# Strassen's weight sums in an FFN: from GpSimd to accumulating transfers and VectorE

## The chip, the cores and the metric

The kernel runs on one core of a Trainium2 chip. The metric is the device time of one execution in microseconds. A core has five engines that concern us here: TensorE (PE, and PEld for its weight loads), VectorE (DVE), ScalarE (ACT), GpSimd (POOL) and SyncE (SP), which issues most transfers between DRAM and on-chip memory. They run side by side and wait for each other through semaphores; each runs its own instructions in order.

## The reference

One layer of a decoder, in float32, for a prompt of 512 tokens and for 8 sequences of one new token each, 520 tokens with shared weights, `D_MODEL` = 2048:

```python
h = modulate(rmsnorm(x, g_norm_mix), sh1, sc1)
x = x + gt1 * (concat([attention(h @ w_in), rwkv7(h @ w_in)]) @ w_out)
h2 = modulate(rmsnorm(x, g_norm_ffn), sh2, sc2)
gate, up = split(h2 @ w_ffn_in, 2)
x = x + gt2 * ((silu(gate) * up) @ w_ffn_out)
y = rmsnorm(x, g_norm_final)
```

The new keys, values and states are returned as well. The change lies in `h2 @ w_ffn_in`, with 2 x 5632 columns in `w_ffn_in`.

## The kernel before

Products are taken in three matmuls: weights and activations are each cut into a high half in TensorE's short float32 format (`wh`, a cast on ScalarE, line 1243) and the rest (`wl`, a subtraction on VectorE, line 1244), and wh·bH, wh·bL and wl·bH are summed in PSUM (`product`, lines 1395 to 1401). The 520 tokens are two halves of `HB` = 260 columns. Activations lie transposed: 128 rows of the model dimension on the partitions, tokens along the free axis.

The FFN's first projection (`ffn_in`) is one level of Strassen's scheme in Winograd's form. The weights of one hidden tile `ht` (128 gate columns and 128 up columns) are four blocks: A11 and A12 (gate, first and second half of the model dimension), A21 and A22 (up). The tokens are four blocks too: B11, B21 (first token half, upper and lower half of the model dimension), B12, B22 (second token half). Instead of eight products of blocks there are seven, over sums:

- sums of weights: S1 = A21 + A22, S2 = S1 - A11, S3 = A11 - A21, S4 = A12 - S2
- differences of tokens: T1 = B12 - B11, T2 = B22 - T1, T3 = B22 - B12, T4 = T2 - B21
- products: A11·B11, A12·B21, S1·T1, S2·T2, S3·T3, A22·T4, S4·B22

The loop runs over 44 hidden tiles and, in each, over two halves `g` of the inner dimension (4 blocks of 128 rows each). Per half SP loads the four blocks of 128x512 weights (256 KB each, `load`: tiles `sr` for A11, A21, A12 with six buffers, `raw` for A22 with three), GpSimd forms the four sums in place (lines 1430, 1431 and 1435, 1436, or 1441, 1442 where the first two products were taken early), and TensorE runs seven products of 12 matmuls, 84 matmuls a half and 168 a tile. The tile names in the program are a11, a21 (first A21, then S1), s3 (with the name tag `ar`), a11 again for S2 and a12 again for S4. At the end of a tile the sums of products (lines 1455 to 1463) are formed on VectorE from PSUM, ScalarE takes the silu (1464), VectorE multiplies (1465), and GpSimd's queue stores the tile of 128x520 in DRAM (`gd`, 1467).

The token differences are formed while the stage starts (`norm_second`): eight pairs of blocks are normalized (VectorE, line 1234; ScalarE, 1238; a small copy on GpSimd, 1236), three of four differences per pair of pairs run on GpSimd (1273, 1278, 1282), one on VectorE (1280), and each result is cut into its two halves. Meanwhile TensorE takes the first two products of hidden tiles 0 to 2, which need only B11 and B21 ("early", 144 matmuls); hidden tiles 0 to 2 then have five products a half.

The order of the instructions on each engine is not the program's order: a scheduler in the tile framework sets it when the kernel is built, from its own prices and from when buffers come free. So an edit in one line can move others. After the stage comes the output projection (`ffn_out`).

Of the kernel before, what the change touches and what calls it, by code (L numbers as in the profile page):

```python
# [10 lines left out]
ALU = mybir.AluOpType  # L11
# [7 lines left out]
HB = 260  # L19
# [44 lines left out]
class Kern:  # L64
# [1197 lines left out]
    def norm_second(self, psum):  # L1262

        nc = self.nc
        r = self.norm(1, psum("ssq2"), nc)
        us = self.norm_start(nc, 1, r)
        yield
        sub = ALU.subtract
        put = lambda f, kp, src: self.cut(nc, f[kp][:, 0], f[kp][:, 1], src)
        for kp in range(4):  # L1270
            b11, b21 = self.hb0[kp], self.hb0[kp + 4]
            b12 = self.norm_pair(nc, 1, kp, r, us)
            nc.gpsimd.tensor_tensor(b11, b12, b11, sub)
            yield
            b22 = self.norm_pair(nc, 1, kp + 4, r, us)
            put(self.T1, kp, b11)
            yield
            nc.gpsimd.tensor_tensor(b12, b22, b12, sub)
            put(self.B22, kp, b22)
            nc.vector.tensor_tensor(b22, b22, b11, sub)  # L1280
            yield
            nc.gpsimd.tensor_tensor(b21, b22, b21, sub)
            put(self.T2, kp, b22)
            yield
            for f, src in ((self.T3, b12), (self.T4, b21)):
                f.append(self.xp.tile([P, 2, 2, HB], F32R, tag="x", bufs=8, name=self.nm("xT")))
                put(f, kp, src)
            yield
# [76 lines left out]
    def ffn_in(self, st):  # L1365

        tc, nc, I = self.tc, self.nc, self.I
        mt = lambda nm: self.ps_m.tile([P, 2, 512], F32, tag="m", name=self.nm(nm))  # L1370
        fb = self.fpb.enter_context(tc.tile_pool(name="fpb", bufs=1, side="right"))
        quads = lambda n: [fb.tile([P, 2, 2, HB], F32R, name=f"{n}_{i}") for i in range(4)]
        self.B22, self.T1, self.T2 = quads("B22"), quads("T1"), quads("T2")
        self.T3, self.T4 = [], []
        plain = lambda k0: lambda k: [a[:, k0 + k] for a in self.B0]
        quad = lambda f: lambda k: [f[k // 2][:, i, k % 2] for i in range(2)]
        B11, B21 = plain(0), plain(8)
        B22, T1, T2, T3, T4 = map(quad, (self.B22, self.T1, self.T2, self.T3, self.T4))
        sp = self.fpb.enter_context(tc.tile_pool(name="strw", bufs=1))
        ct = lambda tag, n: sp.tile([P, 2, HB], F32, tag=tag, bufs=n, name=self.nm(tag))  # L1380
        src = lambda ht, row, col, g: I["w_fi"][2 * ht + row][:, 1024 * col + 512 * g:1024 * col + 512 * g + 512]

        def load(ht, row, col, g, tag="sr"):
            pool, n = (self.w, 3) if tag == "raw" else (sp, 6)
            t = pool.tile([P, 512], F32, tag=tag, bufs=n, name=self.nm(tag))
            nc.sync.dma_start(t, src(ht, row, col, g))
            return t

        def weights(t):
            wh, wl = (self.w.tile([P, 512], F32R, tag=n, bufs=3, name=self.nm(n)) for n in ("wh", "wl"))  # L1390
            self.cut(nc, wh, wl, t)
            return wh, wl

        def product(ps, w, b, g):
            wh, wl = w
            for k in range(4):
                s = slice(k * 128, k * 128 + 128)
                bH, bL = b(4 * g + k)
                for i, (x, y) in enumerate(((wh, bH), (wh, bL), (wl, bH))):
                    nc.tensor.matmul(ps[:, :HB], x[:, s], y, start=g == k == i == 0,  # L1400
                                     stop=g == 1 and k == 3 and i == 2, skip_group_check=True)

        def first_sums(pc, ps):
            nc.scalar.copy(pc[:, 1], ps[:, 0, :HB])
            nc.vector.tensor_tensor(pc[:, 0], ps[:, 1, :HB], pc[:, 1], ALU.add)

        norm = self.norm_second(lambda nm: mt(nm)[:, 0])
        early = []
        for ht in range(3):
            ps = mt("pm")  # L1410
            for g in range(2):
                for col, b in enumerate((B11, B21)):
                    product(ps[:, col], weights(load(ht, 0, col, g, "raw")), b, g)
                    next(norm, None)
            pc = ct("pc", 3)
            first_sums(pc, ps)
            early.append(pc)
        self.kept = []
        for ht in range(FT):
            pc = early.pop(0) if early else None  # L1420
            old = pc is not None
            if not old:
                pc, p12 = ct("pc", 3), mt("pm")
            p45, p67, p3 = mt("pm"), mt("pm"), mt("pm")
            for g in range(2):
                a11, a21 = load(ht, 0, 0, g), load(ht, 1, 0, g)
                a22 = load(ht, 1, 1, g, "raw")
                a12 = load(ht, 0, 1, g)
                s3 = self.w.tile([P, 512], F32, tag="ar", bufs=3, name=self.nm("s3"))
                nc.gpsimd.tensor_tensor(s3, a11, a21, ALU.subtract)  # L1430
                nc.gpsimd.tensor_tensor(a21, a21, a22, ALU.add)  # L1431
                if not old:
                    product(p12[:, 0], weights(a11), B11, g)
                    w2 = weights(a12)
                    nc.gpsimd.tensor_tensor(a11, a21, a11, ALU.subtract)  # L1435
                    nc.gpsimd.tensor_tensor(a12, a12, a11, ALU.subtract)
                    product(p12[:, 1], w2, B21, g)
                    if g == 1:
                        first_sums(pc, p12)
                else:  # L1440
                    nc.gpsimd.tensor_tensor(a11, a21, a11, ALU.subtract)
                    nc.gpsimd.tensor_tensor(a12, a12, a11, ALU.subtract)
                if ht == 0 and g == 0:
                    for _ in range(12):
                        next(norm, None)
                for ps, a, b in ((p45[:, 1], a21, T1), (p67[:, 0], a11, T2), (p67[:, 1], s3, T3),
                                 (p45[:, 0], a22, T4), (p3[:, 0], a12, B22)):
                    product(ps, weights(a), b, g)
                    if ht == 0 and g == 0:
                        next(norm, None)  # L1450
                        next(norm, None)
                    if g == 0:
                        continue
                    if b is T2:
                        nc.vector.tensor_tensor(pc[:, 1], p67[:, 0, :HB], pc[:, 1], ALU.add)
                    elif b is T3:
                        cu = ct("cu", 2)
                        nc.vector.tensor_tensor(cu[:, 1], p67[:, 1, :HB], pc[:, 1], ALU.add)
                    elif b is T4:
                        nc.vector.tensor_tensor(cu[:, 0], cu[:, 1], p45[:, 0, :HB], ALU.subtract)  # L1460
                        nc.vector.tensor_tensor(pc[:, 1], p45[:, 1, :HB], pc[:, 1], ALU.add)  # L1461
                        nc.vector.tensor_tensor(cu[:, 1], p45[:, 1, :HB], cu[:, 1], ALU.add)  # L1462
            nc.vector.tensor_tensor(pc[:, 1], p3[:, 0, :HB], pc[:, 1], ALU.add)  # L1463
            nc.scalar.activation(pc, pc, AF.Silu)
            nc.vector.tensor_tensor(cu, pc, cu, ALU.mult)
            if ht < FT - 4:
                nc.gpsimd.dma_start(self.gd[ht], cu)
            else:
                gs = [self.fp.tile([P, 2, HB], F32R, tag="n", bufs=self.nb, name=self.nm("g" + c)) for c in "HL"]
                self.cut(nc, gs[0], gs[1], cu)  # L1470
                self.kept.append([a.unsqueeze(1) for a in gs])
        self.fpb.close()
# [212 lines left out]
```

## Time and profile before

| | |
|---|---|
| runs of the kernel before | 2715.43, 2715.49, 2721.11 us; median 2715.49 |
| the profiled execution | 2716.84 us |
| its span in the profile | 2714.9 us |
| TensorE busy | 2586.2 us (95%) |
| VectorE busy | 1824.8 us (67%) |
| ScalarE busy | 1109.9 us (41%) |
| GpSimd busy | 808.4 us (30%) |

The profile shows one execution. The time beyond the span, 1.9 us, lies before the first and after the last instruction that it records. Shares of busy time are means over the whole span; matmuls are pipelined, so that their durations of some 280 ns overlap, and how fast TensorE goes is read from how many start in a stretch of time. A wait is put down to the event that came last.

### The profile page before, as it was taken

The numbers are of one execution on the slowest core, as the hardware profiler recorded it, in microseconds if no ns is written. First come the engines' busy times: TensorE is split into PE (matmuls) and PEld (weight loads), VectorE is DVE, ScalarE is ACT, GpSimd is POOL, SyncE is SP. The second block draws the span as 40 slices with busy tenths as digits, with TensorE's granted clock in tenths as the row PEclk, the third lists the DMA queues.
The fourth block names the chain that finished last, engine by engine and source line by source line (L and its number), as shares of the span: only waits on it lengthen the run. The fifth ranks groups of instructions, "written<-read, shape, count | busy, mean of one in ns | idle before, by whom it ended". The sixth has DMA issues, their size and how long they took to land.

```text
span 2714.9 us, 59056 instructions
## 1 busy us (share of the span) xinstructions
PE 2586.2 (95%) x23405; PEld 2369.0 (87%) x23405; DVE 1824.8 (67%) x3637; ACT 1109.9 (41%) x2142; POOL 808.4 (30%) x755
## 2 busy tenths in 40 slices
PE   6899999999999999985999999999999999999997
PEld 4577778788787898885999999999999999999997
DVE  2466677767756364688888888888888863444457
ACT  3133455544423344464444444444444432222225
POOL 0012121211212000066655556555655510000004
PEclk9899999999989998997999999999999999999999
DMA  7965454555556752252333333333333262432433
GB/s 270 326 197 172 139 155 140 154 160 158 158 175 202 235 171 88 96 169 94 132 113 115 109 121 108 116 110 114 117 110 117 98 200 91 125 124 91 125 102 110
DMA packets 203381, 387.24 MB, mean 143 GB/s; under 512 B 29616, under 2 KB 40800, under 8 KB 203072
## 3 DMA queue, kind: packets, MB, share of 16 engines
q1 hardware_dynamic: 193392, 353.10, 40.0%
q0 software_dynamic: 9072, 29.32, 3.5%
q8 instruction: 183, 3.00, 0.4%
q10 hardware_dynamic: 640, 1.05, 0.2%
q14 instruction: 94, 0.77, 0.1%
HBM read 350.92 MB, written 33.46 MB: 142 GB/s over the span
## 4 chain that ended last, share of the span: by engine, by line
PE 45%; DVE 4%; issue 2%; ACT 1%; POOL 1%; DMA 0%; DVEq 0%; SPq 0%; POOLq 0%; ACTq 0%
PE pm L1400 27%; PE pf L98 18%; DVE wl L1244 2%; ACT wh L1243 1%; DVE pc L1463 1%; DVE cu L1460 1%; DVE pc L1461 0%; POOL sr L1435 0%; DMA gr<-gd 0%; POOL sr L1431 0%; DVE x L1546 0%; PE ssq L1214 0%; DVE cu L1462 0%; DVE rstdh L1217 0%; DVEq L1681 0%
## 5 line engine op out<-in xcount | busy, mean ns | idle before, releaser
L1244 DVE TENSOR_TENSOR wl<-sr,wh 128x512 fp32r<-128x512 f32 x428 | 471.1, 1115 | 99.9 <-ACT wh L1243 83.1
L88 ACT CAST wh<-raw 128x512 fp32r<-128x512 f32 (+2 forms) x411 | 250.0, 611 | 496.7 <-PE pf L98 281.0
L1243 ACT CAST wh<-sr 128x512 fp32r<-128x512 f32 x428 | 265.2, 620 | 365.8 <-PE pm L1400 272.1
L98 PE MATMUL pf<-go,wh 128*128 128x260 f32 x2560 | 414.2, 282 | 0.0
L91 DVE TENSOR_TENSOR wl<-raw,wh 128x512 fp32r<-128x512 f32 (+2 forms) x411 | 287.6, 702 | 177.6 <-ACT wh L88 170.9
L98 PEld LDWEIGHTS pf<-go,wh 128*128 128x128 f32 x2560 | 353.9, 188 | 0.1
L98 PE MATMUL pm<-hH,wh 128*128 128x260 f32 (+1 forms) x1248 | 296.7, 317 | 2.0 <-ACT hH L143 1.6
L1400 PE MATMUL pm<-T,wh 128*128 128x260 f32 x1408 | 263.3, 285 | 8.0 <-ACT wh L1243 8.0
L98 PE MATMUL pf<-go,wl 128*128 128x260 f32 x1280 | 267.9, 282 | 0.0
L98 PE MATMUL pm<-hL,wh 128*128 128x260 f32 (+1 forms) x1248 | 264.3, 291 | 0.2 <-DVE hL L144 0.2
L98 PE MATMUL pm<-hH,wl 128*128 128x260 f32 (+1 forms) x1248 | 261.8, 290 | 0.0
L1400 PE MATMUL pm<-xT,wh 128*128 128x260 f32 x1408 | 261.7, 286 | 0.0
L98 PEld LDWEIGHTS pm<-hH,wh 128*128 128x128 f32 (+1 forms) x1248 | 195.1, 191 | 50.6 <-issue 32.0
L1400 PEld LDWEIGHTS pm<-T,wh 128*128 128x128 f32 x1408 | 219.9, 191 | 8.4 <-ACT wh L1243 8.4
L1400 PEld LDWEIGHTS pm<-xT,wh 128*128 128x128 f32 x1408 | 217.1, 189 | 3.9
L1400 PE MATMUL pm<-B0H,wl 128*128 128x260 f32 x704 | 205.7, 292 | 14.3 <-DVE wl L1244 14.3
L1400 PE MATMUL pm<-T,wl 128*128 128x260 f32 x704 | 203.5, 289 | 12.6 <-DVE wl L1244 12.6
L1400 PE MATMUL pm<-B0H,wh 128*128 128x260 f32 x704 | 200.8, 285 | 7.6 <-ACT wh L1243 6.5
L98 PEld LDWEIGHTS pm<-hL,wh 128*128 128x128 f32 (+1 forms) x1248 | 197.1, 191 | 5.6 <-issue 2.3
L98 PEld LDWEIGHTS pm<-hH,wl 128*128 128x128 f32 (+1 forms) x1248 | 197.0, 191 | 5.7 <-issue 1.8
L98 PEld LDWEIGHTS pf<-go,wl 128*128 128x128 f32 x1280 | 201.0, 188 | 0.0
L1400 PE MATMUL pm<-B0L,wh 128*128 128x260 f32 x704 | 199.6, 284 | 0.0
(420 smaller groups left out, 5484.1 us busy)
## 6 DMA issues: line engine op xcount, KB each, us to landing
sr<-in_w_fi SPq DMA_DIRECT2D x264, 256.0 KB, 2.7
ar<-in_w_ada SPq DMA_DIRECT2D x256, 256.0 KB, 3.1
raw<-in_w_fo SPq DMA_DIRECT2D x176, 256.0 KB, 2.6
raw<-in_w_in SPq DMA_DIRECT2D x148, 256.0 KB, 3.6
araw<-in_w_ada SPq DMA_DIRECT2D x64, 512.0 KB, 6.6
raw<-in_w_fi SPq DMA_DIRECT2D x100, 256.0 KB, 3.1
raw<-in_w_out SPq DMA_DIRECT2D x74, 256.0 KB, 3.1
gd<-cu POOLq DMA_DIRECT2D x40, 260.0 KB, 2.7
```

The source lines that it names most:

```text
L88: nc.scalar.copy(wh[:, :n], raw[:, :n])
L91: nc.vector.tensor_tensor(wl[:, :n], raw[:, :n], wh[:, :n].bitcast(F32), ALU.subtract)
L98: nc.tensor.matmul(ps[:m, bank, :HB], w, a[:, k, h, :], start=first and i == 0, stop=last and i == 2, skip_group_check=True,)
L1243: nc.scalar.copy(H, src)
L1244: nc.vector.tensor_tensor(L, src, H.bitcast(F32), ALU.subtract)
L1400: nc.tensor.matmul(ps[:, :HB], x[:, s], y, start=g == k == i == 0, stop=g == 1 and k == 3 and i == 2, skip_group_check=True)
L1460: nc.vector.tensor_tensor(cu[:, 0], cu[:, 1], p45[:, 0, :HB], ALU.subtract)
L1463: nc.vector.tensor_tensor(pc[:, 1], p3[:, 0, :HB], pc[:, 1], ALU.add)
```

## The change

The sums of weights leave GpSimd. S3 is loaded as A11 by SP (new line 1430) and A21 is added to it by a transfer from DRAM that accumulates into on-chip memory (1432); S1 is A21 with A22 added in the same way (1431). Both transfers are issued from GpSimd's queue, and each must wait until its target's first load has landed. S2 and S4 are formed on VectorE (1438, 1439), after the products of A11 and A12 in the program's order. A transfer can only add here, so S3 is now A11 + A21, S2 = S1 + A11 and S4 = A12 + S2: the scheme with the signs of A11 and A12 turned round, and the signs come back in lines 1452, 1455 and 1460. The three token differences of GpSimd run on VectorE.

```diff
@@ norm_second
-            nc.gpsimd.tensor_tensor(b11, b12, b11, sub)
+            nc.vector.tensor_tensor(b11, b12, b11, sub)
...
-            nc.gpsimd.tensor_tensor(b12, b22, b12, sub)
+            nc.vector.tensor_tensor(b12, b22, b12, sub)
...
-            nc.gpsimd.tensor_tensor(b21, b22, b21, sub)
+            nc.vector.tensor_tensor(b21, b22, b21, sub)
@@ ffn_in
                 s3 = self.w.tile([P, 512], F32, tag="ar", bufs=3, name=self.nm("s3"))
-                nc.gpsimd.tensor_tensor(s3, a11, a21, ALU.subtract)
-                nc.gpsimd.tensor_tensor(a21, a21, a22, ALU.add)
+                nc.sync.dma_start(s3, src(ht, 0, 0, g))
+                nc.gpsimd.dma_start(a21, src(ht, 1, 1, g), accum_op=ALU.add)
+                nc.gpsimd.dma_start(s3, src(ht, 1, 0, g), accum_op=ALU.add)
                 if not old:
                     product(p12[:, 0], weights(a11), B11, g)
-                    w2 = weights(a12)
-                    nc.gpsimd.tensor_tensor(a11, a21, a11, ALU.subtract)
-                    nc.gpsimd.tensor_tensor(a12, a12, a11, ALU.subtract)
-                    product(p12[:, 1], w2, B21, g)
+                    product(p12[:, 1], weights(a12), B21, g)
                     if g == 1:
                         first_sums(pc, p12)
-                else:
-                    nc.gpsimd.tensor_tensor(a11, a21, a11, ALU.subtract)
-                    nc.gpsimd.tensor_tensor(a12, a12, a11, ALU.subtract)
+                nc.vector.tensor_tensor(a11, a21, a11, ALU.add)
+                nc.vector.tensor_tensor(a12, a12, a11, ALU.add)
...
                     if b is T2:
-                        nc.vector.tensor_tensor(pc[:, 1], p67[:, 0, :HB], pc[:, 1], ALU.add)
+                        nc.vector.tensor_tensor(pc[:, 1], p67[:, 0, :HB], pc[:, 1], ALU.subtract)
                     elif b is T3:
                         cu = ct("cu", 2)
-                        nc.vector.tensor_tensor(cu[:, 1], p67[:, 1, :HB], pc[:, 1], ALU.add)
+                        nc.vector.tensor_tensor(cu[:, 1], pc[:, 1], p67[:, 1, :HB], ALU.subtract)
...
-            nc.vector.tensor_tensor(pc[:, 1], p3[:, 0, :HB], pc[:, 1], ALU.add)
+            nc.vector.tensor_tensor(pc[:, 1], p3[:, 0, :HB], pc[:, 1], ALU.subtract)
```

Lines of `ffn_in` from 1438 on have lower numbers after the change: the sums at the end of a tile, 1455 to 1463 before, stand at 1452 to 1460, and the multiplication, 1465 before, at 1462.

Three places show how the scheduler's order moves. The first is VectorE at the border of two hidden tiles (8 and 9). `wl` is a cut, `sr` a weight block or a sum in its place, `cu` and `pc` the sums of products of the tile that ends. Before, from the cut of A11 of the new tile on:

```order
L1244 TENSOR_TENSOR wl_17666<-sr_17654,wh_17665 128x512
L1460 TENSOR_TENSOR cu_17608<-cu_17608,pm_17384 128x260
L1461 TENSOR_TENSOR pc_17382<-pm_17384,pc_17382 128x260
L1462 TENSOR_TENSOR cu_17608<-pm_17384,cu_17608 128x260
L1463 TENSOR_TENSOR pc_17382<-pm_17386,pc_17382 128x260
L1244 TENSOR_TENSOR wl_17682<-sr_17660,wh_17681 128x512
L1244 TENSOR_TENSOR wl_17700<-sr_17656,wh_17699 128x512
L1465 TENSOR_TENSOR cu_17608<-pc_17382,cu_17608 128x520
L1244 TENSOR_TENSOR wl_17716<-sr_17654,wh_17715 128x512
```

After the change, the same place:

```order
L1244 TENSOR_TENSOR wl_17685<-sr_17672,wh_17684 128x512
L1457 TENSOR_TENSOR cu_17626<-cu_17626,pm_17400 128x260
L1458 TENSOR_TENSOR pc_17398<-pm_17400,pc_17398 128x260
L1459 TENSOR_TENSOR cu_17626<-pm_17400,cu_17626 128x260
L1460 TENSOR_TENSOR pc_17398<-pm_17402,pc_17398 128x260
L1244 TENSOR_TENSOR wl_17701<-sr_17678,wh_17700 128x512
L1438 TENSOR_TENSOR sr_17672<-sr_17674,sr_17672 128x512
L1462 TENSOR_TENSOR cu_17626<-pc_17398,cu_17626 128x520
L1439 TENSOR_TENSOR sr_17678<-sr_17678,sr_17672 128x512
L1244 TENSOR_TENSOR wl_17719<-sr_17674,wh_17718 128x512
L1244 TENSOR_TENSOR wl_17735<-sr_17672,wh_17734 128x512
```

The cut of A12 (the second `wl`) stands behind the tile's last sum in both. The cut of S1 (the third `wl`), which came next, now comes after the new sums of S2 and S4 and after the multiplication. TensorE's order moves with it: it takes the first two matmuls of S2's product before the third of S1's.

The second place is GpSimd's queue in the same stretch. Before (`gd` is the store of a tile):

```order
L1430 TENSOR_TENSOR s_2530_17662<-sr_17654,sr_17656 128x512
L1431 TENSOR_TENSOR sr_17656<-sr_17656,raw_17658 128x512
L1435 TENSOR_TENSOR sr_17512<-sr_17514,sr_17512 128x512
L1436 TENSOR_TENSOR sr_17518<-sr_17518,sr_17512 128x512
L1430 TENSOR_TENSOR s_2549_17787<-sr_17779,sr_17781 128x512
```

After:

```order
L1432 DMA s_2530_17680<-in_w_fi 128x512
L1464 DMA gd_131<-cu_17357 128x520
L1431 DMA sr_17674<-in_w_fi 128x512
L1432 DMA s_2549_17806<-in_w_fi 128x512
L1431 DMA sr_17800<-in_w_fi 128x512
L1432 DMA s_2574_17949<-in_w_fi 128x512
```

Nothing but transfers is left in it: two that accumulate per half, and one store per tile.

The third place is VectorE at the start of the stage, where the token differences are formed (`hb` is a pair of normalized blocks or a difference). After the change:

```order
L1273 TENSOR_TENSOR hb_14690<-hb_15155,hb_14690 128x520
L1234 TENSOR_TENSOR hb_15275<-x_1593_11649,rstdh_15130 128x2x256
L1278 TENSOR_TENSOR hb_15155<-hb_15179,hb_15155 128x520
L1244 TENSOR_TENSOR T_0_15096<-hb_14690,T_0_15096 128x520
L1244 TENSOR_TENSOR B_0_15092<-hb_15179,B_0_15092 128x520
L1405 TENSOR_TENSOR pc_15208<-pm_15107,pc_15208 128x260
L1280 TENSOR_TENSOR hb_15179<-hb_15179,hb_14690 128x520
L1244 TENSOR_TENSOR xT_15251<-hb_15155,xT_15251 128x520
L1282 TENSOR_TENSOR hb_14802<-hb_15179,hb_14802 128x520
```

Before, the rows of lines 1273, 1278 and 1282 stood on GpSimd. From the reciprocal of line 1217 to the first cut of S1 VectorE has 55 instructions now, and had 42.

## Rows read from the trace of the kernel before

**Rows 1.** The page: busy us, share of the span and instructions of each engine.

```profile
PE 2586.2 (95%) x23405; PEld 2369.0 (87%) x23405; DVE 1824.8 (67%) x3637; ACT 1109.9 (41%) x2142; POOL 808.4 (30%) x755
```

**Rows 2.** Busy us by stretch (columns named in the first row).

```profile
core 0: us, PE busy (x) PEld busy (x) DVE busy (x) ACT busy (x) POOL busy (x), PEclk, DMA share, GB/s
1220.00:1292.50 72.50, 42.48 (x271) 40.02 (x272) 59.51 (x67) 33.86 (x63) 50.35 (x39) 0.76 0.30 98
1292.50:1323.80 31.30, 29.75 (x242) 29.04 (x241) 27.02 (x34) 14.82 (x23) 20.87 (x16) 1.00 0.45 152
1323.80:2190.00 866.20, 851.65 (x6892) 836.50 (x6891) 724.16 (x908) 390.31 (x660) 503.00 (x370) 1.00 0.34 113
2250.00:2600.00 350.00, 350.00 (x2933) 350.00 (x2932) 148.89 (x329) 89.33 (x146) 0.00 (x0) 1.00 0.36 111
...
1256.00:1270.00 14.00, 1.32 (x4) 1.00 (x4) 12.17 (x11) 5.55 (x11) 12.06 (x10) 0.50 0.00 0
1270.00:1292.50 22.50, 18.47 (x117) 18.06 (x118) 18.72 (x21) 8.54 (x15) 13.83 (x9) 0.81 0.29 94
```

**Rows 3.** Weight loads' waits, 1323.8 to 2190 us: total us, times, longest.

```profile
PEld pm L1400 <- DVE wl L1244: 24.2, 47, 1.2
```

**Rows 4.** Chain of waits at a tile's border: start us, us, what.

```profile
1451.99 0.61 DVE wl L1244
...
1452.64 3.42 PE pm L1400 x26
```

**Rows 5.** Timeline of VectorE there: start us, us, line, operation.

```profile
1448.81 1.83 DVE L1244 TENSOR_TENSOR wl<-sr,wh 128x512 fp32r<-128x512 f32 x1
1450.57 0.41 DVE L1460 TENSOR_TENSOR cu<-cu,pm 128x260 f32<-128x260 f32 x1
1450.90 0.41 DVE L1461 TENSOR_TENSOR pc<-pm,pc 128x260 f32<-128x260 f32 x1
...
1454.83 0.68 DVE L1244 TENSOR_TENSOR wl<-sr,wh 128x512 fp32r<-128x512 f32 x1
1455.43 0.68 DVE L1244 TENSOR_TENSOR wl<-s,wh 128x512 fp32r<-128x512 f32 x1
```

**Rows 6.** Timeline of GpSimd there; in brackets idle time before, and its end.

```profile
1447.43 1.29 POOL L1430 TENSOR_TENSOR s<-sr,sr 128x512 f32<-128x512 f32 x1 [3.63 <-DVE wl L1244]
1448.80 1.29 POOL L1431 TENSOR_TENSOR sr<-sr,raw 128x512 f32<-128x512 f32 x1
...
1455.20 0.56 POOL L1467 DMA_DIRECT2D gd<-cu  x1 [0.85 <-DVE cu L1465]
```

**Rows 7.** Groups, 1323.8 to 2190 us: busy us, mean ns, idle before.

```profile
L1244 DVE TENSOR_TENSOR wl<-sr,wh 128x512 fp32r<-128x512 f32 x409 | 449.5, 1114 | 96.2 <-ACT wh L1243 80.0 <-PE pm L1400 1.8
L1465 DVE TENSOR_TENSOR cu<-pc,cu 128x520 f32<-128x520 f32 x41 | 73.4, 1791 | 0.0
L1244 DVE TENSOR_TENSOR wl<-raw,wh 128x512 fp32r<-128x512 f32 x82 | 56.1, 684 | 1.0 <-ACT wh L1243 0.4
```

**Rows 8.** The start: two rows of VectorE's timeline, then one of the chain.

```profile
1223.69 1.77 DVE L1217 RECIPROCAL rstdh<-rstdh 128x260 f32<-128x260 f32 x1
...
1271.58 0.69 DVE L1244 TENSOR_TENSOR T<-hb,T 128x520 fp32r<-128x520 f32 x1
...
1270.01 7.99 PE pm L1400 x45
```

**Rows 9.** Transfers: operation, count, KB each, median us from issue to landing.

```profile
sr<-in_w_fi SPq DMA_DIRECT2D x264, 256.0 KB, 2.7
gd<-cu POOLq DMA_DIRECT2D x40, 260.0 KB, 2.7
x<-x1d POOLq DMA_DIRECT2D x8, 520.0 KB, 5.3
out_vs<-in_cache_v POOLq DMA_DIRECT2D x1, 1016.0 KB, 10.4
```

**Rows 10.** GpSimd's timeline: the first sum for tile 9's first half.

```profile
1437.42 1.28 POOL L1430 TENSOR_TENSOR s<-sr,sr 128x512 f32<-128x512 f32 x1 [2.78 <-DMA sr<-in_w_fi]
```

## The prediction

> **What bounds the kernel now.** The page comes first: TensorE is busy for 95% of the span and VectorE for 67% [rows 1], but a share over the whole program hides stages with different limits, so the second view cuts the FFN's first projection into pieces [rows 2]. In the output projection (2250 to 2600 us), where nothing is in TensorE's way, 2933 matmuls take 350 us: 119.3 ns each. That is the floor. The 41 hidden tiles 3 to 43 take 866.2 us for 6892 matmuls, 125.7 ns each; at the floor they would take 822.4, so 44 us are lost there. The start of the stage (three early tiles and hidden tile 0, 264 matmuls) takes 72.5 us against a floor of 31.5: 41 us are lost. Hidden tiles 1 and 2 take 31.3 against 28.6. In the start the granted clock is 0.76 on average, and 0.50 (1.2 GHz) in the 14 us in which TensorE hardly works. Hence TensorE bounds the stage, with two kinds of holes, and only the holes can be won.
>
> Who makes the holes? In the 41 tiles TensorE's weight loads wait 47 times, 24.2 us in all, for VectorE's low half of a weight block [rows 3], about once per tile. The chain shows where: at the end of each hidden tile VectorE runs the sums at lines 1460 to 1463 and then the cut of A12, and TensorE, two matmuls into A12's product, waits for that cut [rows 4]. VectorE is late because the cut before (A11) took 1.83 us instead of 0.69 [rows 5], and it did so exactly while GpSimd ran its sum of line 1431 [rows 6]. The groups say the same of all tiles: cuts that run beside GpSimd's sums average 1114 ns, those of A22, which don't, 684, and the multiplication of line 1465 takes 1791 ns in the mean [rows 7], where an undisturbed sum of that width takes 0.69 us (1271.58 [rows 8]). So the two engines hold each other up. In the start VectorE is the chain: from the reciprocal at 1223.69 to the cut of the first block for T1 there are 42 instructions in 46.3 us, and TensorE stands until 1270.01 [rows 8].
>
> **The change, part by part.**
>
> *GpSimd's sums go.* Four per half tile, 88 halves, leave GpSimd, as do the 12 differences of token blocks. Their time (1.29 us each [rows 6]) was beside TensorE; what is won is VectorE's pace. An undisturbed 128x512 sum starts every 0.61 us (1454.83, 1455.43 [rows 5]).
>
> *Two sums per half move to VectorE (lines 1438, 1439).* VectorE's load per tile was 724.2/41 = 17.7 us of some 21 [rows 2]. Now: 14 cuts and 4 sums at 0.61, seven PSUM sums at 0.34 (1450.57, 1450.90 [rows 5]), the multiplication at 0.62: 14.0 us. The average falls; the place matters. At the end of a tile the order is now the sum of line 1460, the cut of A12, 1438, the multiplication, 1439, and only then the cut of A21. Take T as TensorE's first matmul of the next tile. Line 1460 waits for the tile's last product and starts at T+0.2; the cut of A12 ends at T+0.2+0.34+0.69 = T+1.2, and is wanted at T+14x0.12 = T+1.7: the old hole closes. The cut of A21 ends at T+0.2+0.34+0.61+0.61+0.62+0.61+0.69 = T+3.7 and TensorE, which first does two matmuls each of T1 and T2, wants it at T+28x0.12 = T+3.4. So a new hole of 0.3 to 0.4 us, plus what the hand-over costs, opens in every tile: I take 0.4, and 41 x 0.4 = 16.4 us. The second half of a tile has room: 1438 and 1439 stand between cuts that come one per product (1.44 us), and use 1.22. The 24.2 us of today's waits go: **41 tiles: -24.2 + 16.4 = -8 us.** A bound below is no new hole (-24), above a hole of 1 us (+17).
>
> *The start.* The same stretch of VectorE now has 55 instructions (13 more: differences and two sums): 48 wide ones at 0.61, three of 0.34, three of 0.14 and the reciprocal of 1.7 make 32.4 us. Following ScalarE's casts beside it, cast by cast, I find some 1.2 us of waits, so the first T1 cut ends near 1257.3 instead of 1270.0: -12.7. From 1270.0 to 1292.5 today 117 matmuls take 22.5 us at a granted 0.81 [rows 2]; 14 us at full clock, 2 for remaining cuts and 2 for a clock that has fallen in the gap make 18: -4.5. **Start: -17 us.** If ScalarE is late oftener, -8; if the clock doesn't fall, -20.
>
> *Two sums become accumulating transfers (lines 1431, 1432).* No row shows one. Below, it costs what a plain transfer does: 2.7 us to landing, on SP as on GpSimd's queue; above, as the GpSimd-queue transfer of twice the bytes, 5.3, or four times, 10.4 [rows 9]. I take 5.3, for it reads two sources per sum. The cover is the prefetch: for the tile that TensorE starts at 1450.36 A11 and A21 have landed by 1437.42, when GpSimd's first sum of them starts [rows 10]; line 1438 wants the sum at T+1.2 = 1451.5. After 1 us of issue in GpSimd's queue (0.56 per DMA [rows 6]) some 13 us are left, and about 10 in the second half, where GpSimd's first sum starts at 1447.43 [rows 6] and line 1438 comes near 1459. Both ends fit. GpSimd's queue holds only these and the store of the hidden tile, none late. If the cover is gone, VectorE stops at line 1438 with all later cuts behind it.
>
> Engine time is the sharper question. The 16 DMA engines are busy 0.34 of 866.2 us [rows 2]: 3.6 us per half for four loads and half a store, 0.8 us per transfer. The change adds a load of A11 into S3 on SP (before A22's and A12's loads, one issue more; SP waits for buffers anyway) and two accumulating transfers. With a price of k plain ones each a half takes (5.5+2k) x 0.8 us: 6.0 at k=1, 7.6 at k=2, of 10.4. Hidden: 0 us. In hidden tiles 1 and 2 a half lasts only 7.2 us, so four halves at 7.6 make 30.4 of today's 31.3: -1. The Trainium skill (Collectives: The Full Stack, "Why ReduceScatter is half of AllGather") says the DMA's add costs no time of its own but two source reads, which halves the rate: by it k=2, as taken. No run here shows it.
>
> *Signs.* Lines 1452, 1455 and 1460 change add for subtract on the same operands: 0.
>
> The sum: -8 - 17 - 1 = -26 against the profiled execution, 2716.84 us (span 2714.9): 2690.8. The median of the runs, 2715.49, lies 1.35 lower: **2690 us** is the forecast.
>
> **Rivals.**
>
> *The transfers fill the DMA engines (slower).* A half lasts 866.2/82 = 10.56 us today. At k=4 it needs 10.8 us of engine time: +0.24 x 82 = 20, which the 18 of the start and of tiles 1 and 2 pay back; from there on the change loses. At k=5 it needs 12.4: +1.84 x 82 = 151, less 18: about 2849. For it: no row has an accumulating transfer. Against: the engines are a third busy today, and plain transfers on GpSimd's queue cost what SP's do. 0.17.
>
> *The wait only moves.* If the new hole is 1 us, the tiles give +17 and the start's gain is eaten: about 2716. For it: six VectorE instructions in a row behind TensorE's last product; against: each was timed undisturbed. 0.11.
>
> *Every hole closes.* Without a hole at T1 and with the full start: 2716 - 24 - 20 - 1 = 2671. 0.10.
>
> *GpSimd's queue starves.* The Trainium skill (SBUF - State Buffer, "Who interferes with whom") has a rule against GpSimd-issued transfers: VectorE can keep GpSimd from writing descriptors. As a mechanism here: each accumulating DMA would wait for a gap in VectorE. But the store of the tile is issued in 0.56 us at 1455.20 while VectorE runs cuts [rows 5, 6] and lands in 2.7 [rows 9]. At 3 us per issue two still fit in a half; only beyond 5 would a half grow: 1 us more is +82 less 18, some 2780. 0.02.
>
> **Numbers.** The forecast has 0.60; its own range is 2678 to 2706. A measurement tells 0.2% (5.4 us) from no change. Faster: 0.60, the closing holes 0.10 and a little of the moved wait, 0.01: 0.71. Same: most of the moved wait, 0.09. Slower: the filled DMA engines, the starved queue and 0.01: 0.20. The range reaches from the closing holes to the mild filled case and leaves out its far end: 2670 to 2728.
>
> **What would show it.** Right: A cuts near 690 ns in all groups; the chain's hole at T1's third matmul instead of A12's; the first T1 cut near 1257; DMA share near 0.7 in the tiles; line 1438 never waiting for a landing. Wrong: line 1438 waiting for a DMA in most tiles, a DMA share over 0.95, or a start that still lasts 70 us.

## The result, and the profile after

Five executions of the changed kernel took 2687.29 to 2703.30 us, median 2698.61; the kernel before took 2715.43 in the median of five. The ratio is 0.9929, with a 95% interval of 0.9910 to 0.9947: 14 to 24 us faster, where 25.5 were forecast. The profiled execution took 2703.30 us, span 2701.5.

The page of the changed kernel: busy time by engine (answers to [rows 1]), and the DMA queues with packets, MB and share of 16 engines.

```profile
PE 2585.5 (96%) x23405; PEld 2370.4 (88%) x23405; DVE 1710.3 (63%) x3825; ACT 1113.6 (41%) x2142; POOL 421.4 (16%) x567
q1 hardware_dynamic: 206064, 376.18, 43.2%
q0 software_dynamic: 34416, 75.47, 13.7%
```

VectorE has 188 instructions more and is busy 114 us less: the ones that stayed became shorter. The same stretches as in [rows 2], cut at the first matmul of hidden tiles 1, 3 and of the output projection:

```profile
core 0: us, PE busy (x) PEld busy (x) DVE busy (x) ACT busy (x) POOL busy (x), PEclk, DMA share, GB/s
1221.00:1281.20 60.20, 42.20 (x271) 40.27 (x271) 50.22 (x85) 34.27 (x63) 11.14 (x18) 0.80 0.55 152
1281.20:1321.30 40.10, 32.20 (x242) 31.65 (x241) 22.26 (x40) 14.75 (x23) 8.11 (x10) 0.91 0.71 190
1321.30:2175.60 854.30, 847.47 (x6890) 833.22 (x6890) 623.74 (x1070) 393.58 (x659) 163.41 (x205) 1.00 0.73 188
2230.00:2580.00 350.00, 350.00 (x2933) 350.00 (x2932) 149.00 (x329) 89.55 (x146) 0.00 (x0) 1.00 0.36 111
```

The start gained 12.3 us (72.5 to 60.2), the 41 tiles 11.9 (866.2 to 854.3), and **hidden tiles 1 and 2 lost 8.8** (31.3 to 40.1). The three make -15.4. The rest of the program took 2 us more in this execution, without a change there.

A tile's border, in the timeline of TensorE (one row) and VectorE. The first matmul of tile 9 starts at 1446.36:

```profile
1446.36 0.28 PE L1400 MATMUL pm<-B0H,wh 128*128 128x260 f32 x1
1446.56 0.43 DVE L1460 TENSOR_TENSOR pc<-pm,pc 128x260 f32<-128x260 f32 x1
1446.91 0.68 DVE L1244 TENSOR_TENSOR wl<-sr,wh 128x512 fp32r<-128x512 f32 x1
1447.51 0.68 DVE L1438 TENSOR_TENSOR sr<-sr,sr 128x512 f32<-128x512 f32 x1
1448.11 0.69 DVE L1462 TENSOR_TENSOR cu<-pc,cu 128x520 f32<-128x520 f32 x1
1448.72 0.69 DVE L1439 TENSOR_TENSOR sr<-sr,sr 128x512 f32<-128x512 f32 x1
1449.32 1.29 DVE L1244 TENSOR_TENSOR wl<-sr,wh 128x512 fp32r<-128x512 f32 x2
```

Everything runs at its undisturbed pace of 0.61 us, where [rows 5] had a cut of 1.83. The groups of the 41 tiles say the same (busy us, mean ns, idle before; compare [rows 7]):

```profile
L1244 DVE TENSOR_TENSOR wl<-sr,wh 128x512 fp32r<-128x512 f32 x409 | 279.2, 690 | 92.7 <-ACT wh L1243 82.5
L1462 DVE TENSOR_TENSOR cu<-pc,cu 128x520 f32<-128x520 f32 x41 | 28.4, 693 | 0.0
```

Hidden tiles 1 and 2 are another matter. The timeline of the changed kernel there, by engine:

```profile
1285.84 0.88 POOL L1431 DMA_DIRECT2D sr<-in_w_fi  x1
1289.89 0.62 ACT L1243 CAST wh<-raw 128x512 fp32r<-128x512 f32 x1 [0.83 <-PE pm L1400]
1287.66 0.69 DVE L1244 TENSOR_TENSOR wl<-sr,wh 128x512 fp32r<-128x512 f32 x1 [0.74 <-ACT wh L1243]
1292.66 0.69 DVE L1438 TENSOR_TENSOR sr<-sr,sr 128x512 f32<-128x512 f32 x1 [4.31 <-DMA sr<-in_w_fi]
1293.27 0.68 DVE L1244 TENSOR_TENSOR wl<-s,wh 128x512 fp32r<-128x512 f32 x1
1293.88 0.69 DVE L1439 TENSOR_TENSOR sr<-sr,sr 128x512 f32<-128x512 f32 x1
1294.48 0.68 DVE L1244 TENSOR_TENSOR wl<-raw,wh 128x512 fp32r<-128x512 f32 x1
1295.22 0.39 PE L1400 MATMUL pm<-xT,wl 128*128 128x260 f32 x1 [3.56 <-DVE wl L1244]
```

Read it from below. TensorE stood 3.56 us for the low half of an A22 block (`raw`), whose cut VectorE began only at 1294.48. ScalarE had cast that block by 1290.51, so it had landed long before. But VectorE's next instruction was line 1438 for the next half tile, and that waited 4.31 us for an accumulating transfer issued at 1285.84. What stood behind it, the cut of S3 (`s`), line 1439 and the cut of A22, could not pass. The same happens once more in tile 2 (4.30 us) and once at the end of tile 0 (3.2 us). The chain of waits shows what the sum in tile 2 waited for:

```profile
1288.38 6.64 DMA sr<-in_w_fi
...
1295.58 6.45 DMA sr<-in_w_fi
...
1302.05 0.04 DVE sr L1438
```

The plain load of A21 took 6.64 us to land, and the transfer that adds A22 to it another 6.45.

### The profile page after: what moved, and what is told of

Its sections match the earlier page's. It is cut to its first block, busy times and chain, and to the rows that moved or that the text cites. A ratio compares the mean times of both kernels' runs of the same rounds, so it can differ in the third digit from the quotient of the medians.

```text
span 2701.5 us, 59274 instructions
## 1 busy us (share of the span) xinstructions
PE 2585.5 (96%) x23405; PEld 2370.4 (88%) x23405; DVE 1710.3 (63%) x3825; ACT 1113.6 (41%) x2142; POOL 421.4 (16%) x567
## 4 chain that ended last, share of the span: by engine, by line
PE 74%; DVE 6%; DMA 3%; issue 2%; ACT 2%; POOL 0%; SPq 0%; DVEq 0%; ACTq 0%; POOLq 0%
PE pm L1400 32%; PE pf L98 18%; PE pm L98 10%; PE po L98 5%; PE psc L49 2%; PE ada L310 2%; DVE wl L1244 1%; DVE wl L91 1%; DMA raw<-in_w_out 1%; PE pl L49 1%; DVE stmp L49 1%; DMA sr<-in_w_fi 1%; PE pO L49 1%; PE pt L49 1%; ACT Z L49 1%
## 5 line engine op out<-in xcount | busy, mean ns | idle before, releaser
L1244 DVE TENSOR_TENSOR wl<-sr,wh 128x512 fp32r<-128x512 f32 x428 | 292.2, 690 | 96.8 <-ACT wh L1243 86.3
L1400 PE MATMUL pm<-B0H,wl 128*128 128x260 f32 x704 | 199.6, 284 | 1.2 <-DVE wl L1244 1.2
```

The lines of the kernel that those rows point to most:

```text
L1244: nc.vector.tensor_tensor(L, src, H.bitcast(F32), ALU.subtract)
```

## The experiments

The table holds each kernel's stretches between the same matmuls, in us, from its own profiled execution. "Stage from" is where the stage's first matmul stands in the span. With the first, the kernel before had a median of 2715.43 us; on the chips of the others 2723.74 (e1, e2, e3, e5), 2720.53 (e4, e7, e8), 2721.33 (e9, e10, e0) and 2714.67 (e12, e14). So compare ratios and stretches, not times.

| kernel | stage from | start | tiles 1, 2 | tiles 3 to 43 | ratio to before |
|---|---|---|---|---|---|
| before | 1220.0 | 72.5 | 31.3 | 866.2 | 1 |
| the change | 1221.0 | 60.2 | 40.1 | 854.3 | 0.9929 |
| e0 the change again | 1221.9 | 61.4 | 37.8 | 853.9 | 0.9931 (0.9906 to 0.9957) |
| e1 differences only | 1223.1 | 65.1 | 32.4 | 868.9 | 0.9954 (0.9935 to 0.9972) |
| e2 sums only | 1217.5 | 63.5 | 36.6 | 854.1 | 0.9918 (0.9899 to 0.9937) |
| e3 S2, S4 on GpSimd | 1223.4 | 61.8 | 31.1 | 849.1 | one execution |
| e4 no accumulating | 1227.7 | 57.8 | 31.7 | 885.5 | 1.0013 (0.9998 to 1.0028) |
| e5 plain twin | 1223.3 | 54.9 | 33.4 | 854.1 | one execution |
| e7 order of loads | 1217.2 | 61.4 | 36.6 | 854.3 | one execution |
| e8 cut of S1 first | 1219.1 | 60.4 | 41.1 | 841.2 | 0.9880 (0.9856 to 0.9904) |
| e9 tiles 0 to 2 on GpSimd | 1220.3 | 61.9 | 32.3 | 855.1 | one execution |
| e10 e8 and e9 | 1215.4 | 57.6 | 30.8 | 843.2 | 0.9855 (0.9832 to 0.9877) |
| e14 e10, differences on GpSimd | 1222.7 | 66.3 | 31.1 | 842.2 | one execution |
| e12 e10, cut of S2 sooner | 1219.6 | 58.8 | 31.0 | 836.4 | 0.9833 (0.9788 to 0.9877) |

**e1, e2: the two parts alone.** e1 is the kernel before with lines 1273, 1278 and 1282 on VectorE:

```diff
-            nc.gpsimd.tensor_tensor(b11, b12, b11, sub)
+            nc.vector.tensor_tensor(b11, b12, b11, sub)
```

> Only the 12 differences of token blocks move to VectorE; the weight sums stay on GpSimd. Theory: the start of the stage is long because VectorE and GpSimd hand the differences to and fro, so it falls from 72.5 us to 60 to 64; hidden tiles 1 and 2 stay at 31.3 and tiles 3 to 43 at 866.2, since their sums are as before. About 2705 us, a ratio near 0.996. Rival (the start is shorter because GpSimd's weight sums leave): the start stays above 70 us and the ratio at 1.000.

e2 is the changed kernel with these lines back on GpSimd.

> Only the weight sums change (two accumulating transfers, two sums on VectorE); the 12 differences of token blocks stay on GpSimd. Theory: tiles 3 to 43 take 854 us as in the changed kernel, tiles 1 and 2 about 40, and the start stays near 70: about 2708 us, ratio 0.997. Rival (the weight sums shorten the start): the start near 60 and the ratio at 0.993, as with the whole change.

e1 came out near its theory (start 65.1, a little above; the tiles not shorter). In e2 the theory fell: the start went to 63.5, and the ratio can't be told from that of the whole change. In the kernel before, GpSimd's weight sums stand among its differences, here three of them ahead of a difference (line 1273):

```profile
1259.95 1.27 POOL L1431 TENSOR_TENSOR sr<-sr,raw 128x512 f32<-128x512 f32 x1
1261.30 1.60 POOL L1441 TENSOR_TENSOR sr<-sr,sr 128x512 f32<-128x512 f32 x1
1262.98 1.60 POOL L1442 TENSOR_TENSOR sr<-sr,sr 128x512 f32<-128x512 f32 x1
1264.54 1.72 POOL L1273 TENSOR_TENSOR hb<-hb,hb 128x520 f32<-128x520 f32 x1
```

Either part alone shortens the start (by 7.4 and 9.0 us), and the two overlap: 0.46% and 0.82% alone, 0.71% together. The tiles' gain belongs to the sums alone.

**e3: what stretched the cuts.**

```diff
-                nc.vector.tensor_tensor(a11, a21, a11, ALU.add)
-                nc.vector.tensor_tensor(a12, a12, a11, ALU.add)
+                nc.gpsimd.tensor_tensor(a11, a21, a11, ALU.add)
+                nc.gpsimd.tensor_tensor(a12, a12, a11, ALU.add)
```

> The changed kernel with S2 and S4 (lines 1438, 1439) back on GpSimd; the accumulating transfers stay. Theory: what stretched VectorE's cuts before was a GpSimd sum beside them, so with two sums a half the cuts of sr blocks average 750 to 900 ns, between 690 (changed kernel) and 1114 (before), and some cuts stand at 1.1 us or more at a tile's border. VectorE has 2.4 us less work at a border, so tiles 3 to 43 can come out anywhere from 20.4 to 21.0 us each. Rival (the accumulating transfers or SBUF traffic in general set the pace of the cuts): the cuts stay near 690 ns.

Groups of VectorE in tiles 3 to 43 of e3:

```profile
L1244 DVE TENSOR_TENSOR wl<-sr,wh 128x512 fp32r<-128x512 f32 x409 | 385.2, 959 | 113.4 <-ACT wh L1243 103.6
L1462 DVE TENSOR_TENSOR cu<-pc,cu 128x520 f32<-128x520 f32 x41 | 73.8, 1799 | 0.0
```

Two GpSimd sums a half bring back most of the stretch (959 ns of 690 to 1114), more than expected, with the accumulating transfers in place as in the changed kernel; the rival falls. Yet in e3 VectorE never waits for a transfer in tiles 1 and 2, at a higher load of the DMA engines than the changed kernel's 0.71:

```profile
1285.20:1316.30 31.10, 29.59 (x243) 29.11 (x242) 22.48 (x35) 14.73 (x23) 16.00 (x15) 1.00 0.87 229
```

So the DMA engines did not bound these tiles. And the 41 tiles are 5.2 us shorter than in the changed kernel, although the cuts are longer: in the order that the change got, S2 and S4 on VectorE cost more there than they save. They pay only with another order (e8).

**e5: the price of accumulating.**

```diff
-                nc.gpsimd.dma_start(a21, src(ht, 1, 1, g), accum_op=ALU.add)
-                nc.gpsimd.dma_start(s3, src(ht, 1, 0, g), accum_op=ALU.add)
+                nc.gpsimd.dma_start(a21, src(ht, 1, 1, g))
+                nc.gpsimd.dma_start(s3, src(ht, 1, 0, g))
```

> The changed kernel with its two accumulating transfers a half replaced by plain ones of the same blocks to the same places on the same queue; S1 then holds A22 and S3 holds A21, so that part of the scheme is left out. Theory: an accumulating transfer costs two plain ones in engine time, so the DMA share in tiles 3 to 43 falls from 0.73 to 0.57, and from issue to landing 5.5 us falls to about 3; the waits in hidden tiles 1 and 2 (two of 4 us) are plain load and then accumulating transfer in series and shrink to about half: the two tiles fall from 40.1 to 34 to 36 us, and tiles 3 to 43 stay at 854. Rival (the add costs nothing, the waits are only the second transfer's place behind the first): share stays above 0.70 and tiles 1 and 2 above 38.

Of the twin, tiles 3 to 43 by the windows view, its software queue on the page, and its transfers (median us to landing last):

```profile
1311.60:2165.70 854.10, 847.25 (x6890) 833.00 (x6890) 623.48 (x1070) 393.49 (x659) 110.43 (x205) 1.00 0.58 189
```

```profile
q0 software_dynamic: 23152, 75.47, 8.4%
s<-in_w_fi POOLq DMA_DIRECT2D x88, 256.0 KB, 3.6
sr<-in_w_fi POOLq DMA_DIRECT2D x88, 256.0 KB, 3.7
```

And the same two groups of the changed kernel:

```profile
s<-in_w_fi POOLq DMA_DIRECT2D x88, 256.0 KB, 5.5
sr<-in_w_fi POOLq DMA_DIRECT2D x88, 256.0 KB, 4.7
```

The queue's engine time is 0.137 x 2701.5 = 370 us against 0.084 x 2691.4 = 226 for the same bytes: 144 us over 176 transfers, 0.82 us each, one plain transfer's price on top. Landing takes 1 to 2 us longer. Tiles 3 to 43 don't notice. Tiles 1 and 2 and the start are 6.7 and 5.3 us shorter. VectorE stands 3.8 us at line 1438 in these tiles instead of 8.6, and 1.3 us in the start instead of 3.2; where the rest comes from is not shown.

**e4: without accumulating transfers.**

```diff
-                nc.sync.dma_start(s3, src(ht, 0, 0, g))
-                nc.gpsimd.dma_start(a21, src(ht, 1, 1, g), accum_op=ALU.add)
-                nc.gpsimd.dma_start(s3, src(ht, 1, 0, g), accum_op=ALU.add)
+                nc.vector.tensor_tensor(s3, a11, a21, ALU.add)
+                nc.vector.tensor_tensor(a21, a21, a22, ALU.add)
```

> The changed kernel without accumulating transfers: S1 and S3 are formed on VectorE from the plain loads, like S2 and S4; 176 transfers a run fall away and 176 sums of 0.61 us come to VectorE. Theory: VectorE has room (14.0 + 4 x 0.61 = 16.4 us of 20.8 a tile), nothing waits for a second transfer any more, so tiles 1 and 2 fall from 40.1 to 31 to 33 us; tiles 3 to 43 stay at 20.8 to 21.1 each, as the hole at T1 is set by the instructions behind the tile's last product; the start loses 1 to 3 us to the four more sums. About 10 us below the changed kernel as profiled: a ratio to the kernel before near 0.990. Rival (the accumulating transfers are what frees VectorE, and without them it falls behind): tiles 3 to 43 above 21.4 each and a ratio above 0.995.

Tiles 1 and 2 came as expected, and the start is 2.4 us shorter instead of longer; the 41 tiles are 31 us longer than the changed kernel's, the rival's figures. But VectorE does not run out of time there: it is busy for 80% (706.6 of 885.5 us). Its waits for transfers, and all waits of TensorE's weight loads, from 1317 on (total us, times, longest):

```profile
DVE s L1430 <- DMA sr<-in_w_fi: 31.1, 45, 2.1
PEld pm L1400 <- DVE wl L1244: 26.5, 89, 1.0
PEld pm L1400 <- DVE pc L1451: 23.8, 38, 2.2
```

VectorE stands at the next half's first sum (line 1430) until its plain load lands, and in 40 of the 41 tiles the instruction behind it is line 1451, the reading of PSUM for which TensorE waits. VectorE stands 18.3 us just ahead of it, most of these 23.8: the mechanism of tiles 1 and 2 again, now in nearly every tile. The waits for cuts grew too, to 26.5 us from the changed kernel's 15.4, with two more sums per half among the cuts. What the accumulating transfers buy is that a sum does not stand in an engine's order.

**e7: the loads of the serial pair first** (A21 and S3's first load with their accumulating transfers ahead of A11, A22 and A12):

```diff
-                a11, a21 = load(ht, 0, 0, g), load(ht, 1, 0, g)
-                a22 = load(ht, 1, 1, g, "raw")
-                a12 = load(ht, 0, 1, g)
+                a21 = load(ht, 1, 0, g)
...
+                a11 = load(ht, 0, 0, g)
+                a22 = load(ht, 1, 1, g, "raw")
+                a12 = load(ht, 0, 1, g)
```

> The changed kernel with the loads that get a second transfer (A21, and A11 into S3) and the two accumulating transfers put ahead of the loads of A11, A22 and A12. Theory: the serial pair starts one to three loads earlier, 1 to 3 us, so the two waits of 4 us in tiles 1 and 2 shrink but do not vanish: 40.1 falls to 34 to 38; tiles 3 to 43 stay at 854. Rival (buffers alone set when the pair starts): tiles 1 and 2 stay at 39 to 41.

36.6 us, within the forecast. But the changed kernel itself took 37.8 in its second execution (e0, below), and VectorE stands at these sums for 7.5 us here and 8.2 there, so that a gain from the order of loads is not shown; the waits stay. Whether more buffers for the blocks would take them away stays open: with eight instead of six (e6) the pool needs 26.2 KB of each partition, of 22.3 that are left, so that there is no room even for one more.

**e8: the hole at S1.** The cut of S1 is written ahead of the sums (`weights` makes the two halves of a block):

```diff
+                w1 = weights(a21)
                 nc.vector.tensor_tensor(a11, a21, a11, ALU.add)
                 nc.vector.tensor_tensor(a12, a12, a11, ALU.add)
...
-                    product(ps, weights(a), b, g)
+                    product(ps, w1 if b is T1 else weights(a), b, g)
```

> The changed kernel with the cut of S1 written ahead of the two sums of lines 1438 and 1439, so that behind a tile's last product VectorE runs line 1460, the cut of A12, the cut of S1, the multiplication, the two sums, the cut of S2, and TensorE takes S1's twelve matmuls before S2's. Theory: the hole of 0.33 + 0.10 us at S1's third matmul is the queue of sums ahead of its cut, so it closes: 20.84 falls to 20.37 to 20.45 us a tile, 854 to 836 to 839. Tiles 1 and 2 and the start within 4 us of the changed kernel: ratio near 0.987. Rival (the hole moves on to S2's cut): 20.7 to 20.9 a tile.

841.2 us, 13.1 less: the hole was the queue ahead of that cut. It is 2 us above the expected span; 0.10 us a tile is left, a gap of 0.22 us instead of 0.12 at the matmul that needs S2's cut.

**e9, e10, e0: the order on VectorE.** e9 takes the sums off VectorE's order in the three tiles with short halves only (there `old` is true); e10 joins e8 and e9:

```diff
-                nc.vector.tensor_tensor(a11, a21, a11, ALU.add)
-                nc.vector.tensor_tensor(a12, a12, a11, ALU.add)
+                (nc.gpsimd if old else nc.vector).tensor_tensor(a11, a21, a11, ALU.add)
+                (nc.gpsimd if old else nc.vector).tensor_tensor(a12, a12, a11, ALU.add)
```

> The changed kernel with S2 and S4 on GpSimd in hidden tiles 0 to 2 alone. Theory: the two waits in tiles 1 and 2 come from VectorE's order: line 1438 of the next half stands ahead of cuts whose data landed long before, and holds them until its accumulating transfer lands. With the sum on GpSimd VectorE passes: tiles 1 and 2 fall from 40.1 to 31 to 32 us at a DMA share near 0.87, the start stays at 60 to 63, tiles 3 to 43 at 854. Rival (the landing itself is late for TensorE, whoever forms the sum): tiles 1 and 2 stay above 37.

> The changed kernel with both: the cut of S1 ahead of the sums, and S2 and S4 of tiles 0 to 2 on GpSimd. Theory: the gains lie in different stretches and add up: tiles 1 and 2 at 31 to 32 us, tiles 3 to 43 at 841, start 60 to 63; about 8 us below the kernel with the cut first alone, a ratio to the kernel before of 0.984 to 0.986. Rival (the time saved early comes back as a wait later): tiles 3 to 5 longer than 21 us and the ratio at 0.988.

> The changed kernel itself once more, on the same chip as the two before it. Theory: the stages repeat: start 58 to 62, tiles 1 and 2 38 to 42, tiles 3 to 43 854.3; ratio 0.991 to 0.995. Rival (the waits in tiles 1 and 2 were an accident of one execution): the two tiles near 31.

e0 repeats the change, waits included (37.8 us, just under the expected span). In e9 tiles 1 and 2 take 32.3 us. The transfers land no sooner: now GpSimd stands at line 1438 for them, three times (total us, times, longest):

```profile
POOL sr L1438 <- DMA sr<-in_w_fi: 13.3, 3, 4.9
```

But no cut stands behind it there: what cost TensorE its time was the order on VectorE. The two gains add up in e10:

```profile
1273.00:1303.80 30.80, 29.60 (x242) 29.05 (x241) 22.49 (x35) 14.65 (x23) 15.05 (x14) 1.00 0.89 230
1303.80:2147.00 843.20, 841.13 (x6891) 832.37 (x6890) 630.05 (x1070) 389.73 (x659) 164.94 (x207) 1.00 0.75 192
```

Its ratio is 0.9855, as expected. Some 2 us come back in tile 3 (22.5 us where the next ones take 20.5), the first whose sums are on VectorE again.

**e14, e12: what the differences are worth, and the last gap.** e14 is e10 with the differences on GpSimd. e12 is e10 with S2's cut written ahead of S4's sum, and the old tile's silu, multiplication and store (`finish`) behind the next tile's product with T2:

```diff
                 (nc.gpsimd if old else nc.vector).tensor_tensor(a11, a21, a11, ALU.add)
+                w2 = weights(a11)
                 (nc.gpsimd if old else nc.vector).tensor_tensor(a12, a12, a11, ALU.add)
...
+                    if late and g == 0 and b is T2:
+                        finish(*late)
+                        late = None
```

> The kernel with both edits (cut of S1 first, S2 and S4 of tiles 0 to 2 on GpSimd), but with the 12 token differences back on GpSimd. With the waits of tiles 1 and 2 in place the differences on VectorE were worth nothing: the start and tiles 1 and 2 together took 100.1 us with the sums alone and 99 to 100 with the whole change. Theory: they were worth nothing because the time saved came back as those waits; without the waits they are worth 5 to 10 us, so the start and tiles 1 and 2 take 93 to 99 us here, against 88.4 with both. Rival (GpSimd forms the differences as fast once its sums are gone): 87 to 90 us.

> The kernel with both edits, and at a tile's border the multiplication of the old tile written behind S2's sum, S2's cut ahead of S4's sum. Theory: of the 20.48 us of a tile 0.10 is the wait for S2's cut (the gap of 0.22 us at the 39th matmul); S2's sum comes 0.61 us sooner, so the gap goes if its cut follows: 20.37 a tile, 836 to 839 us for tiles 3 to 43. Rival (the cut keeps its place behind S4's sum): 20.48 a tile, no change against the kernel with both.

e14 needs 97.4 us for the start and tiles 1 and 2, e10 88.4. The differences on VectorE, worth nothing beside the waits (e2 100.1, the change 100.3), are worth 9 us without them (8 against e12, 89.8). These are single executions, and e9, also with the differences on VectorE and without these waits, has 94.2, so the size is uncertain. e12 closes the gap, though the order of S2's cut and S4's sum did not change: S2's sum starts 0.61 us sooner, with the multiplication between the two sums, and its cut ends 0.25 us sooner. Its tiles 3 to 43:

```profile
1309.40:2145.80 836.40, 835.75 (x6890) 829.61 (x6890) 623.28 (x1070) 389.59 (x659) 163.95 (x206) 1.00 0.74 194
```

With 0.9833 it is the fastest version here, some 26 us below the change by the ratios; against e10 the intervals overlap, so that step is shown by the stretch and not by the time.

## Why the prediction was right, and where not

By stretches, -15.4 us came where -26 was forecast: the 41 tiles gave 3.9 more than worked out, the start 4.7 less, and hidden tiles 1 and 2 lost 8.8 instead of gaining 1. That the tiles' surplus hid part of the two misses was luck.

- **What bounds the kernel, and who makes the holes: right.** With GpSimd's sums gone, VectorE's cuts fell from 1114 to 690 ns and the multiplication from 1791 to 693; with two of four sums e3 brought back 959 and 1799. The Trainium skill (SBUF - State Buffer, "Who interferes with whom") says that a VectorE instruction with two SBUF inputs contends with a GpSimd instruction that reads SBUF. The trace agrees: the cuts and the multiplication read two blocks each, and they are the ones that went from 690 to 1114 ns and from 693 to 1791 beside GpSimd's sums.
- **The 41 tiles: the new hole right to 0.02 us, the sum -11.9 instead of -8.** Line 1460 started at T+0.20, A12's cut ended at T+1.23, S1's at about T+3.65, all as worked out. The weight loads wait 41 times, 15.4 us in all (0.38 each, where 0.4 was taken). By that view -8.8 would have come; the other 3 us lie in short gaps between matmuls that it does not count in full (209 of 0.14 to 0.4 us before, 123 after), so the 24.2 of [rows 3] was a little small.
- **The start: -12.3 instead of -17.** VectorE's 55 instructions ran within 0.6 us of their price, but the reciprocal began at 1224.59, 0.9 us later than before, and the chain had 2.5 us of waits instead of 1.2, so TensorE got S1's cut at 1260.18 and not 1257.3. The remaining stretch took 21.0 us instead of 18, mainly because line 1438 waited 3.2 us for its transfer: TensorE stood 2.54 us behind it.
- **The transfers: the price was right, the cover was not.** An accumulating transfer costs two plain ones (0.82 us more each; share 0.73 in the tiles, near 0.7 forecast), and lands in 4.7 to 5.5 us in the median (5.3 taken), but in up to 6.8 in tiles 1 and 2. The Trainium skill (Collectives: The Full Stack, "Why ReduceScatter is half of AllGather") has the DMA's add cost a second source read; the trace agrees with k=2. In the 41 tiles line 1438 never waits, as forecast.
- **The step that failed is "hidden tiles 1 and 2: -1".** It counted engine time (7.6 us a half) and let the transfers flow. But the plain load (6.64 us in the chain above), the accumulating transfer (6.45) and the sum come one after the other, for a half that lasts 7.2 us; and "VectorE stops at line 1438 with all later cuts behind it", which the prediction named as the price of a lost cover, happened just there, three times. It read the order only at the border of a late tile, where a half lasts 10.4 us. It cost 9 us in tiles 1 and 2 and 3 in the start. That VectorE's order is the cause is shown by e9 (the waits for the same transfers stand on GpSimd, and the tiles are short again) and by e3; why the scheduler puts the next half's sum so early was not tried.
- **The rivals.** The DMA engines did not fill (they carry 0.87 to 0.89 in e3 and e10), and GpSimd's queue did not starve, though an accumulating issue took 0.85 to 1.0 us instead of 0.54 in the plain twin.

## What to carry to other kernels

Moving a sum to an engine that runs in order moves its wait there too: before an operation that waits for a transfer is placed on a busy engine, read what stands behind it on that engine, in the shortest loop as well as in the typical one. Engine time says whether transfers fit, not whether they come in time. And two savings that feed the same wait don't add up (e1 and e2), until that wait is gone (e14, in one execution).

## What was not expected

The weight sums alone shortened the start as much as the differences did: GpSimd's two kinds of work had held each other up. Executions differ before the stage begins, in code that no kernel here touches: its first matmul stands at 1215.4 to 1227.7 us of the span, more than most of these edits are worth, so that the stretches tell more than single times. In e4, 176 sums more on VectorE cost 31 us in the tiles, though it was idle a fifth of the time.
